# Token rows kept in f32 until they are transposed, a router that reads the residual, and a bias table and scan phases made on 128 partitions

## The chip, the cores and the metric

The kernel runs on one core of a Trainium2 chip. The core has a matrix engine (TensorE, PE; its weight loads are shown as PEld), a vector engine (VectorE, DVE), an activation engine (ScalarE, ACT), a general engine (GpSimd, POOL) and SyncE (SP), which here only issues transfers. Each engine takes its instructions in order, and semaphores hold an instruction back until what it needs is done. Sixteen DMA engines move data between the memory of the chip (DRAM) and the core. The metric is the time of one execution in microseconds (us); lower is better.

## The reference

One layer of a hybrid decoder, 512 tokens of 1,024 channels, all in f32. Cut to what matters:

```python
h = rms_norm(x, norm1_g)
proj = h @ w_in                      # 1024 -> 2048, columns split among three mixers
y_ssm  = ssm_mixer(proj[:, :256])    # complex diagonal state space, 16 groups, 64 states each, GELU, GLU
y_pool = pool_mixer(proj[:, 256:512])            # causal means over windows 2, 4, 8, 16
y_att  = moba_attention(q, k, v, rel_bias)       # 8 heads x 64, causal, with T5 bias per head and distance
x = x + concat(y_ssm, y_pool, y_att) @ w_out
h = rms_norm(x, norm2_g)
g_sel  = argmax(h @ group_w + group_b)           # one of 4 groups of experts
top2   = top_k(h @ router_w[g_sel] + router_b, 2)  # two of its 4 experts
x = x + sum over the two: weight * ((silu(h @ w_gate[e]) * (h @ w_up[e])) @ w_down[e])
out = rms_norm(x, final_norm_g)
```

The state space mixer multiplies its states by a fixed complex number per step, exp(lambda*dt). The kernel needs the powers of that number, as magnitude and phase.

## The kernel before

**Precision.** Products that must be as good as f32 are made of f16 halves: a value is kept as a high part (f16 of the value) and a low part (f16 of the rest), and three products (`PASSES`: high x high, low x high, high x low) are added in PSUM. A weight comes from DRAM as f32 into one of five staging slots (token `stg`), ACT writes the high half and DVE (sometimes POOL) the low half (`split_steps`, line 390), and the slot is free. Small things, attention and the state space are done in f32.

**Order.** Every engine's instructions stand in an order that a planner (`Flow`, lines 99 to 273) works out when the kernel is built. The work is written as generators that yield the engine, the events they need and the tokens they take; the planner holds a cost model of each instruction (lines 128 to 176) and takes, engine by engine, the piece that it believes can start first, with a rank as a handicap. A token such as `stg`, `mm` or `xT` is a place in a ring of buffers. On the chip only the order and the semaphores are left: if a transfer is slower than its model, all that stands behind the waiting instruction on that engine waits too.

**Stages.**

1. *First norm and projections* (`s_norm1`, `s_units`). x is normed, transposed on PE and split. Eight projections of 256 columns follow in the order v0, u, q0, k0, p, q1, k1, v1 (line 452). u feeds the state space, p the pooling, the others attention. `s_unit_loads` (455) brings their weights.
2. *State space* (`s_prep` 577, `s_prep_b` 633, `s_prep_e` 663, `s_prep_c` 702, `s_ssm` 905). Tokens are taken in 64 chunks of 8. DVE makes the unit's sine and cosine and then the powers 0 to 8 by complex doubling (`pw`). POOL makes the phases of chunk 0 to 63 by doubling (`eph`) and corrects their length (`nrm2`, `epn`). PE makes the chunk inputs (`pv`); DVE turns them by the phases (`z`), scans them with the magnitude `r8t`, and DVE and POOL turn them back (`unwind`). `dm` is a table that goes through DRAM (`kp_scr`).
3. *Bias table* (`s_bias`, 767). A one-hot product on PE gives a row of 639 bias values for each of 8 heads, on 8 partitions (`bv`). It is written 64 times to DRAM (`t_scr`), each copy one longer, so that reading it back with a shorter step gives every partition its row shifted by one (`tb`, eight reads). Attention (`s_attend`, 1086) needs `tb`.
4. *Clears* (`s_clear`, 800). `x_scr`, where token rows are gathered by expert slot, and the first rows of `y_scr` are written with zeros, 20 transfers of 512 KB.
5. *w_out and second norm* (`s_wout`, `x2_out`, `s_norm2` 1227). For each of four token tiles m, DVE adds the product to the residual in two halves (`x2_t[m]`); POOL and DVE multiply it by norm2_g (`xg`), PE transposes that, ACT copies it (`h2T`).
6. *Router* (`s_route`, 1265). PE makes the 20 logits; DVE scales them by the token's rms, finds the group and the two experts, and with a triangular product each token's place in its expert's 96 slots (`slot_i`). `hl_out` (1497) makes the scaled row's f16 halves, and POOL scatters these rows to `x_scr` by two indirect transfers per tile. The 16 x 96 slots are 12 units of 128. For units 0 and 1 (`NG = 2`) DVE also makes one-hot matrices (`sel`), and PE gathers the rows, already transposed, from the halves on the core (`gather`: banks `gb` for unit 0, `gc` for unit 1).
7. *Experts* (`s_xt`, `s_gate_up`, `s_down`). From unit 2 on a unit's rows are read back (`xr`), transposed on PE as 16 f16 blocks, and copied to `xT`. The gate and up products follow (`pg`), then silu, a transpose, the down product (`py`), and a scatter to `y_scr`. Expert weights come in a stream of 512 KB loads; the pages into which they are split are freed by earlier stages and units (`GU_FREE`, `DN_FREE`, events such as `dstart`).
8. *End*: rows of `y_scr` are added to the residual, normed and written.

Of the kernel before, what the change touches and what calls it, by code (L numbers as in the profile page):

```python
# [19 lines left out]
P = 128  # L20
# [13 lines left out]
NB = 32  # L34
TW = 576
# [28 lines left out]
C_W = C_JUNK + 12  # L64

# [210 lines left out]
def hybrid_trunk_kernel(tc, a, out, cap=CAPACITY, dbg=None):  # L276
# [6 lines left out]
    NG = 2  # L283
# [30 lines left out]
    x_scr = dram.tile([NSLOT + 2 * S, 2 * D], F16, name="x_scr")  # L314
# [5 lines left out]
    t_scr = dram.tile([8, HD * (VW + 1)], F32, name="t_scr")  # L320
# [44 lines left out]
    rbias = gp_.tile([P, 20], F32, name="rbias")  # L365
    ap_ = pool_of(phE, "ap_", 1, "right")
# [44 lines left out]
    def s_first_loads():  # L411
# [14 lines left out]
        sp.dma_start(spar, a["ssm_par"])  # L426
        sp.dma_start(sd, a["ssm_dl"])
# [121 lines left out]
    def cmul_p(rr, ii, ar, ai, br, bi, shape, nai=None, nbi=None):  # L549

        t_ = shaped(tmp_p, shape)
        tt = pool.tensor_tensor
        tt(t_, ai, bi, ALU.mult)
        tt(rr, ar, br, ALU.mult)
        tt(rr, rr, t_, ALU.subtract)
        tt(t_, ai if nai is None else nai, br, ALU.mult)
        tt(ii, ar, bi if nbi is None else nbi, ALU.mult)
        tt(ii, ii, t_, ALU.add)

# [5 lines left out]
    eph = (s1a[:, 0:512].rearrange("p (g c) -> p g c", g=GH), s1b[:, 1152:1664].rearrange("p (g c) -> p g c", g=GH))  # L565
    epn = prep.tile([P, 2, GH, NCH], F32, name="epn")
    nrm2 = prep.tile([P, GH, NCH], F32, name="nrm2")
# [9 lines left out]
    def s_prep():  # L577
        dt, ar_dt, th, er, r8, n_, thr, absn, us, uc = (sm() for _ in range(10))
# [3 lines left out]
        v.tensor_tensor(ar_dt, are, dt, ALU.mult)  # L582
        v.tensor_tensor(th, aim, dt, ALU.mult)
        yield "act"
        act.activation(er, ar_dt, AF.Exp)
        act.activation(r8, ar_dt, AF.Exp, scale=float(T))
        yield "dve"
        magic = 12582912.0
        v.tensor_scalar(n_, th, 1.0 / (2 * PI), magic, ALU.mult, ALU.add)
        v.tensor_scalar(n_, n_, -magic, None, ALU.add)  # L590
        c1 = 6.28125
        c2 = float(np.float32(2 * PI - c1))
        v.scalar_tensor_tensor(thr, n_, -c1, th, ALU.mult, ALU.add)
        v.scalar_tensor_tensor(thr, n_, -c2, thr, ALU.mult, ALU.add)
        lim = 3.1415925
        v.tensor_scalar(thr, thr, lim, -lim, ALU.min, ALU.max)
        v.scalar_tensor_tensor(absn, thr, -1.0, thr, ALU.mult, ALU.max)
        yield "act", ("rs",)
        act.activation(us, thr, AF.Sin)
        act.activation(uc, absn, AF.Sin, bias=hpi, scale=-1.0)  # L600
        e1["unit"] = (uc, us)
        e1["r8"] = r8
        fl.sig("unit")

        m2, t_, wre, wim, lm1, ire, iim = (sm() for _ in range(7))
# [7 lines left out]
        yield "dve"  # L613
        v.memset(pw[:, 0, 0, :], 1.0)
        v.memset(pw[:, 1, 0, :], 0.0)
        v.tensor_tensor(pw[:, 0, 1, :], er, uc, ALU.mult)
        v.tensor_tensor(pw[:, 1, 1, :], er, us, ALU.mult)
        for n in (1, 2, 4):
            yield "dve"
            cmul(pw[:, 0, n + 1:2 * n + 1, :], pw[:, 1, n + 1:2 * n + 1, :],  # L620
                 pw[:, 0, 1:n + 1, :], pw[:, 1, 1:n + 1, :],
                 pw[:, 0, n:n + 1, :].to_broadcast([P, n, GH]),
                 pw[:, 1, n:n + 1, :].to_broadcast([P, n, GH]), [n, GH])
# [39 lines left out]
    def s_prep_e():  # L663

        yield "pool"
        pool.memset(bbd, 0.0)
        yield "pool", ("unit", "rs")
        er_, ei_ = e1["unit"]
        for _ in range(3):
            yield "pool"  # L670
            nr, ni = sm(), sm()
            cmul_p(nr, ni, er_, ei_, er_, ei_, [GH])
            er_, ei_ = nr, ni
        yield "pool"
        pool.memset(eph[0][:, :, 0:1], 1.0)
        pool.memset(eph[1][:, :, 0:1], 0.0)
        n = 1
        while n < NCH:
            yield "pool"
            cmul_p(eph[0][:, :, n:2 * n], eph[1][:, :, n:2 * n], eph[0][:, :, 0:n], eph[1][:, :, 0:n],  # L680
                   bc3(er_, n), bc3(ei_, n), [GH, n])
            if 2 * n < NCH:
                yield "pool"
                nr, ni = sm(), sm()
                cmul_p(nr, ni, er_, ei_, er_, ei_, [GH])
                er_, ei_ = nr, ni
            n *= 2
        fl.sig("eph")
        tt = pool.tensor_tensor
        t_ = shaped(tmp_p, [GH, NCH])  # L690
        yield "pool"
        tt(nrm2, eph[0], eph[0], ALU.mult)
        tt(t_, eph[1], eph[1], ALU.mult)
        tt(nrm2, nrm2, t_, ALU.add)
        yield "dve"
        v.tensor_scalar(nrm2, nrm2, -1.0, 2.0, ALU.mult, ALU.add)
        yield "pool"
        tt(epn[:, 0], eph[0], nrm2, ALU.mult)
        tt(epn[:, 1], eph[1], nrm2, ALU.mult)
        fl.sig("epn")  # L700
# [197 lines left out]
    def v_out(ps, b, t):  # L898
        yield "act"
        act.activation(v_sb[:, t, b * 256:(b + 1) * 256], ps[:, 0:256], AF.Copy, scale=ISC)  # L900
        fl.give("mm")
        fl.sig(("v", b, t))


    def s_ssm():
        XT = {"wa": xs_[0], "wb": xs_[1], "zt": xs_[2], "U": xs_[3], "glw": xs4}

# [1184 lines left out]
```

## Time and profile before

| | us |
|---|---|
| median of three runs | 452.4 |
| lowest and highest of them | 450.56, 454.28 |
| profiled execution, its own time | 451.55 |
| its span, first to last instruction | 449.7 |
| mean granted PE clock in it | 0.933 |

| engine | busy us | instructions |
|---|---|---|
| PE | 377.0 | 3,472 |
| DVE | 321.9 | 655 |
| ACT | 245.9 | 397 |
| POOL | 106.0 | 183 |

| what moves | |
|---|---|
| in all | 109.84 MB, mean 244 GB/s |
| read from DRAM, written to it | 83.56 MB, 25.67 MB |

Busy time is an average over stages with different limits. A busy engine is not the bound by itself: what counts is which wait ends last in a stage. Nearly every instruction has line 91, the helper that records it, so a group is known by its tiles: `px<-wo,cat` is the w_out product, `pg<-gu,xts` an expert's gate and up product. The tile names are those of the buffer's first owner (`xp` is the page of x, later used by the scan, the residual and the rows that are scattered; `sm_r` holds the router's small values).

A row of a timeline reads: start, length, engine, line, operation, written tile, read tiles, shape, count of merged instructions, and in brackets the idle time of that engine before it and who ended it. A row of waits reads: who waited, for whom, us in total, times, the longest.

### The profile page before, as it was taken

To read this page: it belongs to the slowest core of one execution; us is meant where nothing else is said; L and a number is where in the kernel's file an instruction comes from. 1 tells how busy PE (TensorE), PEld (TensorE's weight loads), DVE (VectorE), ACT (ScalarE), POOL (GpSimd) and SP (SyncE) were. 2 spreads that over 40 slices of the span, in tenths; PEclk is the share of its full clock that TensorE was granted. 3 is DMA by queue.
4 is the path that set the end of the run, shared out by engine and by line. 5 is a ranking of instruction groups with operands and counts; after the bars stand their busy time and mean duration, and the time that the engine had idled before them with its cause. 6 is when DMAs were issued, how large, how long until landed. Compare 5 with 4: busy or idle time off the path is not lost. (4 is left out here: it accounts for less than half of the span.)

```text
span 449.7 us, 8913 instructions
## 1 busy us (share of the span) xinstructions
PE 377.0 (84%) x3472; PEld 209.2 (47%) x3472; DVE 321.9 (72%) x655; ACT 245.9 (55%) x397; POOL 106.0 (24%) x183
## 2 busy tenths in 40 slices
PE   2899963399998999999899758989999796596992
PEld 1697531164445556444455556545444342242341
DVE  2789805955673786788589998488877786796382
ACT  4752203143564994876677423387667777475131
POOL 1248985402300000000325561010302002000010
PEclk9999995779999999999999967999999898598997
DMA  8912548996796389675477697547899997989943
GB/s 279 348 50 38 73 51 222 382 383 218 238 143 209 99 247 390 211 233 188 140 232 279 253 353 288 185 149 218 276 415 364 377 361 284 316 284 339 349 164 142
DMA packets 48816, 109.84 MB, mean 244 GB/s; under 512 B 4195, under 2 KB 25443, under 8 KB 48772
## 3 DMA queue, kind: packets, MB, share of 16 engines
q1 hardware_dynamic: 45620, 99.57, 68.8%
q0 software_dynamic: 2592, 9.44, 5.2%
q8 instruction: 28, 0.46, 0.4%
q10 hardware_dynamic: 560, 0.25, 0.3%
q14 instruction: 16, 0.13, 0.1%
HBM read 83.56 MB, written 25.67 MB: 243 GB/s over the span
## 5 line engine op out<-in xcount | busy, mean ns | idle before, releaser
L91 DVE SCALAR_TENSOR_TENSOR gu<-st_lde,gu 128x1024 f16<-128x1024 f32 x56 | 69.4, 1255 | 16.9 <-ACT gu L91 16.8
L91 PE MATMUL pg<-gu,xts 128*32 128x512 f16 (+1 forms) x912 | 65.3, 395 | 7.1 <-ACT gu L91 7.0
L91 ACT ACTIVATE gu<-st_lde 128x1024 f16<-128x1024 f32 x56 | 58.4, 1055 | 23.2 <-DMA st_lde<-in_moe_w_gate_dram 13.8
L91 PEld LDWEIGHTS <-xts 128*32 128x32 f16 (+1 forms) x912 | 28.1, 102 | 40.2 <-issue 17.1
L91 PE MATMUL px<-wo,cat 128*128 128x512 f16 x192 | 44.9, 379 | 0.8 <-DVE xp L91 0.8
L91 PE MATMUL py<-dn,aT 128*32 128x512 f16 (+1 forms) x480 | 39.4, 413 | 4.6 <-ACT aT L91 3.2
L91 DVE SCALAR_TENSOR_TENSOR dn<-st_lde,dn 128x1024 f16<-128x1024 f32 x31 | 37.1, 1218 | 3.0 <-ACT dn L91 2.8
L91 POOL DMA_INDIRECT y_scr<-ys,tok x10 | 12.3, 1234 | 103.1 <-ACT ys L91 82.7
L91 ACT ACTIVATE dn<-st_lde 128x1024 f16<-128x1024 f32 x32 | 33.7, 1058 | 3.9 <-DMA st_lde<-in_moe_w_down_dram 3.4
L91 PEld LDWEIGHTS <-hT 128*64 128x64 f16 (+1 forms) x384 | 31.3, 156 | 7.0 <-issue 2.7
L91 PE MATMUL ps_k<-hT,w_k 128*128 128x512 f16 x96 | 23.3, 395 | 10.8 <-ACT qk L91 10.8
L91 ACT ACTIVATE pr<-pr,nm 128x128 f32<-128x128 f32 (+3 forms) x32 | 17.9, 559 | 23.7 <-DVE nm L91 23.4
L91 POOL TENSOR_TENSOR xg<-xp,g 128x512 f32<-128x512 f32 x4 | 6.1, 1513 | 97.2 <-DVE nm L91 92.7
L91 PEld LDWEIGHTS <-cat 128*128 128x128 f16 x192 | 18.2, 99 | 22.8 <-issue 4.9
L91 PEld LDWEIGHTS <-aT 128*32 128x32 f16 (+1 forms) x480 | 14.5, 105 | 25.8 <-issue 6.6
L91 PE MATMUL ps_v<-w_v,hT 128*128 128x256 f16 x192 | 25.3, 290 | 0.9 <-ACT hT L91 0.5
L91 ACT COPY pts<-ptp 128x128 f32<-128x128 f32 (+3 forms) x32 | 13.3, 423 | 19.7 <-PE ptp L91 19.4
L91 PE MATMUL psS<-qk 64*64 64x128 f32 (+3 forms) x128 | 23.9, 472 | 0.0
L91 PE MATMUL ptp<-cpk,pr 128*128 128x128 f32 x80 | 14.4, 288 | 10.0 <-DVE rcp L91 7.4
L91 PE MATMUL ps_q<-hT,w_q 128*128 128x512 f16 x96 | 22.7, 379 | 0.0
L91 PEld LDWEIGHTS <-w_k 128*128 128x128 f16 x96 | 9.2, 100 | 23.1 <-issue 13.9
L91 PEld LDWEIGHTS ptp<-cpk,pr 128*128 128x128 f32 x80 | 9.4, 142 | 18.2 <-issue 12.6
(265 smaller groups left out, 721.5 us busy)
## 6 DMA issues: line engine op xcount, KB each, us to landing
st_lde<-in_moe_w_down_dram SPq DMA_DIRECT2D x32, 512.0 KB
st_lde<-in_moe_w_gate_dram SPq DMA_DIRECT2D x28, 512.0 KB
st_lde<-in_moe_w_up_dram SPq DMA_DIRECT2D x28, 512.0 KB
x_scr<-zero SPq DMA_DIRECT2D x12, 512.0 KB
xr<-x_scr SPq DMA_DIRECT2D x10, 512.0 KB
xp<-in_x_dram SPq DMA_DIRECT2D x8, 512.0 KB
y_scr<-zero SPq DMA_DIRECT2D x8, 512.0 KB
yr<-y_scr SPq DMA_DIRECT2D x4, 1024.0 KB
```

Source lines behind the costliest of these rows:

```text
L91: r = f(*args, **kw)
```

## The change

*Bias table.* The one-hot product's left side is widened to 8 heads x 16 copies, so that the table stands on all 128 partitions. It is written once (16 copies per head), and eight reads of 16 partitions each fill `tb`. The loads of `small` and `pool_w` move behind the write.

*Scan phases.* `s_prep` works out the phase of every chunk and the magnitude and phase of every power from one product: the step's angle in turns, split into an exact high part and a rest, times a row of multipliers (`mul`, 73 columns: 0 to 63, then 0 to 8 eighths), reduced to half a turn, then one sine and one cosine on ACT over 584 columns. The doubling on DVE and on POOL, `nrm2` and `epn` go; the unwinding uses the same phases. Projection p waits for `bl` instead of `cl`, and the mixer's gate weights are loaded ahead (`s_glw`).

*Clears.* The planner takes one at a time (token `clr`), from the start of projection u instead of k0.

*Router.* The transposes read `x2_t` itself; norm2_g is multiplied into the router's weights (`rw`). DVE makes the scaled row once, in f32, over the residual (`s_xs`); that row is scattered as it is, so `x_scr` holds f32 rows of the same 4 KB. Slots are worked out before the one-hot matrix, and the scatter is its own piece (`s_scatter`).

*Units.* Only unit 0 is gathered on PE (`NG = 1`), by eight f32 products per tile. Unit 1 is read back like the later ones, into the residual page of the last tile. Transposed blocks are f32, and the halves are split after the transpose (`parts_out`: ACT the high, DVE the low part). All units use two `xT` buffers in turn.

```diff
-    NG = 2
+    NG = 1
...
-    x_scr = dram.tile([NSLOT + 2 * S, 2 * D], F16, name="x_scr")
+    x_scr = dram.tile([NSLOT + 2 * S, D], F32, name="x_scr")
...
-    t_scr = dram.tile([8, HD * (VW + 1)], F32, name="t_scr")
+    t_scr = dram.tile([1, 8 * NC * (VW + 1)], F32, name="t_scr")
...
+        x, y = (w.rearrange("p (g c) -> p g c", g=GH) for w in (scr_b[:, 0:GH * NPH], s1b[:, 1152:1152 + GH * NPH]))
+        mulb = mul.unsqueeze(1).to_broadcast([P, GH, NPH])
         magic = 12582912.0
...
+        v.tensor_tensor(x, mulb, bc3(uh, NPH), ALU.mult)
+        v.tensor_scalar(y, x, magic, None, ALU.add)
+        v.scalar_tensor_tensor(x, y, -magic, x, ALU.add, ALU.subtract)
+        yield "dve"
+        v.tensor_tensor(y, mulb, bc3(ul, NPH), ALU.mult)
+        v.tensor_tensor(x, y, x, ALU.subtract)
+        v.tensor_scalar(y, x, magic, None, ALU.add)
+        v.scalar_tensor_tensor(x, y, -magic, x, ALU.add, ALU.subtract)
+        v.scalar_tensor_tensor(y, x, -1.0, x, ALU.mult, ALU.max)
         yield "act", ("rs",)
...
+        act.activation(ph[1], x, AF.Sin, scale=-TURN)
+        act.activation(ph[0], y, AF.Sin, bias=hpi, scale=-TURN)
+        fl.sig("unit", "eph")
...
     def s_prep_e():
-
         yield "pool"
         pool.memset(bbd, 0.0)
-        yield "pool", ("unit", "rs")
...
-        while n < NCH:
-            yield "pool"
-            cmul_p(eph[0][:, :, n:2 * n], eph[1][:, :, n:2 * n], eph[0][:, :, 0:n], eph[1][:, :, 0:n],
-                   bc3(er_, n), bc3(ei_, n), [GH, n])
...
+        v.tensor_copy(rbx.rearrange("p (h c) -> p h c", c=NC), rb.unsqueeze(2).to_broadcast([NB + 1, 8, NC]))
...
-            pe.matmul(pb[0:8, 0:c1 - c0], rb, oh[:, c0:c1], start=True, stop=True)
+            pe.matmul(pb[:, 0:c1 - c0], rbx, oh[:, c0:c1], start=True, stop=True)
...
-        sp.dma_start(t_scr.rearrange("h (p w) -> h p w", p=HD), bv.unsqueeze(1).to_broadcast([8, HD, VW + 1]))
+        sp.dma_start(t_scr[0].rearrange("(p w) -> p w", w=VW + 1), bv)
...
+        for j in range(2):
+            for r in range(0, HD, NC):
+                sp.dma_start(tb[j * HD + r:j * HD + r + NC], bass.AP(
+                    t_scr.tensor, t_scr.offset + j * NC * (VW + 1) + HD - 1 - r,
+                    [[VW, NC], [2 * NC * (VW + 1), NPAIR], [1, TW]]))
...
+            yield "sp", ("zero", ("start", "u")), ("clr",)
...
+        v.tensor_tensor(rw, rw, g2c.unsqueeze(2).to_broadcast([P, KD, 20]), ALU.mult)
...
-                pe.transpose(pt[:, i * P:(i + 1) * P], xg[:, k * P:(k + 1) * P], ident)
+                pe.transpose(pt[:, i * P:(i + 1) * P], x2_t[m][:, k * P:(k + 1) * P], ident)
...
+    def s_xs(m, rs16):
+
+        yield "dve", ("rest",) + ((("acc", m), ("h2T", m, 1)) if m < NT - 1 else ())
+        xs = xs_m[m] = x2_t[m] if m < NT - 1 else M["R"].tile([P, D], F32, name="xs3")
+        for nh in range(2):
+            if nh:
+                yield "dve"
+            half = slice(nh * 512, (nh + 1) * 512)
+            v.scalar_tensor_tensor(xs[:, half], x2_t[m][:, half], rs16, g2_t["g"][:, half], ALU.mult, ALU.mult)
+        fl.sig(("xs", m))
+
+    def parts_out(u, h, ps, end):
+
+        yield "act"
+        hi, lo = (xT_[u][:, i * KD + 4 * h:i * KD + 4 * h + 4, :] for i in range(2))
+        src = ps.rearrange("p (k n) -> p k n", k=4)
+        act.copy(hi, src)
+        yield "dve"
+        v.tensor_tensor(lo, src, hi, ALU.subtract)
+        end()
...
+            pe.matmul(M["gb"][k // 4][:, (k % 4) * P:(k % 4 + 1) * P], src[:, k], M["sel"][:, m, 0],
+                      start=(m == 0 and k % 4 == 0), stop=(m == NT - 1 and k % 4 == 3))
...
-    DN_FREE = ("prep", "s1", ("end", "k1"), ("end", "v1"), ("wo_end", 0), ("gather", NG - 1, NT - 1), ("gup", 1))
+    DN_FREE = ("prep", "s1", ("end", "k1"), ("end", "v1"), ("wo_end", 0), ("gather", 0, NT - 1), ("xT", 1))
...
+            yield "sp", (("B",) if u > NG else ()) + tuple(("scatd", m) for m in range(NT)) + (("acc", NT - 1),), ("xr",)
+
+            xr = x2_t[NT - 1] if u == NG else B["ex"].tile([P, D], F32, tag="xr", name=f"xr{u}")
             sp.dma_start(xr, x_scr[u * P:(u + 1) * P, :])
```

`hl_out`, `gather`, `gathered` and `s_gather_all` go.

More of the change, by code (lines that the diff above doesn't have):

```diff
@@ L34 @@
 NB = 32
+NC = 16
+NPH = NCH + T + 1
 TW = 576
@@ L564, in hybrid_trunk_kernel @@
     bb = prep.tile([P, 2, GH, H], F32, name="bb")
[L565 to L567 removed]
+    ph = [prep.tile([P, GH, NPH], F32, name=f"ph{i}") for i in range(2)]
+    eph = [x[:, :, 0:NCH] for x in ph]
+    mag = prep.tile([P, GH, T + 1], F32, name="mag")
+    mul = prep.tile([P, NPH], F32, name="mul")
     r8t = prep.tile([P, GH, NCH], F32, name="r8t")
@@ L595, in s_prep, with halves @@
-        lim = 3.1415925
-        v.tensor_scalar(thr, thr, lim, -lim, ALU.min, ALU.max)
-        v.scalar_tensor_tensor(absn, thr, -1.0, thr, ALU.mult, ALU.max)
-        yield "act", ("rs",)
[L599 to L605, printed above, removed]
+        def halves(hi, x):
+            v.tensor_scalar(t_, x, 4097.0, None, ALU.mult)
+            v.tensor_tensor(u_, t_, x, ALU.subtract)
+            v.tensor_tensor(hi, t_, u_, ALU.subtract)
@@ L902, in v_out, with s_glw @@
         fl.sig(("v", b, t))
+    GLW = []
+    def s_glw():
+        yield "sp", ("rs", ("start", "k0"))
+        GLW.append(xs4.rearrange("p (a b) -> p a b", a=2))
+        for gp in range(2):
+            sp.dma_start(GLW[0][:, gp, :], a["glu_w"][gp])
+        fl.sig_dma("glw")
     def s_ssm():
@@ L969, in s_ssm @@
         fl.sig("sprev")
-        glw = sw([P, 2, 256], "glw")
-        for gp in range(2):
-            sp.dma_start(glw[:, gp, :], a["glu_w"][gp])
-        fl.sig_dma("glw")
+        glw = GLW[0]
         y_sb = sw([P, T, GH, H], "zt")
@@ L1411, in s_gather @@
[L1411 to L1432 removed]
+    xs_m = {}
@@ new lines, in unit_end, with end, s_gather @@
+    def unit_end(u, h, tag, left):
+        def end():
+            fl.give(tag)
+            left[0] -= 1
+            if not left[0]:
+                fl.sig(("xT", u))
+        return end
+    def s_gather(m):
+        yield "pe", ((("sel", m - 1), ("gather", 0, m - 1)) if m else (("wo_end", 1),)) + (("xs", m),), () if m else ("mm", "mm")
+        if m == 0:
+            M["gb"] = [bank("mm", f"gb{i}") for i in range(2)]
+        src = xs_m[m].rearrange("p (c k) -> p k c", k=KD)
+        for k in range(KD):
+            if k == 4:
+                yield "pe"
+            pe.matmul(M["gb"][k // 4][:, (k % 4) * P:(k % 4 + 1) * P], src[:, k], M["sel"][:, m, 0],
+                      start=(m == 0 and k % 4 == 0), stop=(m == NT - 1 and k % 4 == 3))
+        fl.sig(("gather", 0, m))
+        if m == NT - 1:
+            xT_[0] = xts[0]
+            left = [2]
+            for h in range(2):
+                fl.spawn(0, parts_out(0, h, M["gb"][h], unit_end(0, h, "mm", left)))
@@ L1434, in unit_in @@
     def unit_in(u):
-        return xts[(u - 1) % NXT]
+        return xts[u % NXT]
     def s_gates():
```

296 lines of the change are left out of this document (95 added, 201 removed).

## The prediction

> **What bounds the kernel now.** I read the busy table of the page, then busy time by stretch, then the waits, then each engine's timeline where TensorE (PE) stood still.
> ```profile
> PE 377.0 (84%) x3472; PEld 209.2 (47%) x3472; DVE 321.9 (72%) x655; ACT 245.9 (55%) x397; POOL 106.0 (24%) x183
> ```
>
> PE is busy for 84% of the span, so the question is which of its pauses the change can touch. Two lie early. In the stretches below the columns are the stretch, its length, the busy time and count of PE, PEld, DVE, ACT and POOL, then PE's granted clock, the DMA share and GB/s.
>
> ```profile
> 41.00:69.00 28.00, 22.91 (x232) 13.41 (x231) 13.29 (x12) 6.37 (x11) 25.49 (x50) 0.99 0.52 70
> 63.90:74.70 10.80, 0.03 (x2) 0.02 (x1) 2.19 (x3) 2.65 (x4) 9.38 (x9) 0.70 0.67 147
> 74.70:82.70 8.00, 8.00 (x32) 3.09 (x31) 7.95 (x12) 1.23 (x1) 1.18 (x2) 0.76 1.04 322
> 82.70:90.10 7.40, 0.03 (x1) 0.00 (x0) 7.22 (x14) 1.58 (x5) 4.08 (x3) 0.68 1.09 385
> 90.10:101.00 10.90, 10.85 (x62) 7.12 (x62) 5.72 (x14) 4.67 (x12) 0.14 (x2) 0.75 1.09 384
> ```
>
> PE is empty for 10.8 and 7.4 us, and in the two working stretches beside these it is granted only about three quarters of its clock. The waits between 56 and 92 us, and SP's between 35 and 80, say who is late:
>
> ```profile
> ACT w_p L91 <- DMA st_ld_p<-in_w_in_dram: 14.8, 2, 13.4
> DVE nrm L91 <- POOL nrm L91: 14.3, 1, 14.3
> PE ps_k L91 <- ACT qk L91: 10.8, 1, 10.8
> PE ptp L91 <- DVE rcp L91: 7.4, 1, 7.4
> SPq L91 <- DMA t_scr<-scr: 21.9, 1, 21.9
> ```
>
> The engine timelines give the chains:
>
> ```profile
> 58.56 5.35 PE L91 MATMUL ps_k<-hT,w_k 128*128 128x512 f16 x24
> 40.71 0.86 SPq L91 DMA_DIRECT2D t_scr<-scr  x1
> 41.68 5.50 SPq L91 DMA_DIRECT2D st_ld_p<-in_w_in_dram  x2
> 69.12 5.10 SPq L91 DMA_DIRECT2D tb<-t_scr  x8
> 74.05 0.58 ACT L91 ACTIVATE qk<-ps_k 128x512 f32<-128x512 f32 x1
> 71.83 2.27 POOL L91 TENSOR_TENSOR epn<-s1b,nrm 128x512 f32<-128x512 f32 x1
> 76.59 0.68 DVE L91 TENSOR_TENSOR xp<-pv,s 128x512 f32<-128x512 f32 x1
> 80.18 2.33 DVE L91 TENSOR_TENSOR_SCAN xp<-r8t,xp 128x512 f32<-128x512 f32 x2
> 85.78 1.62 DVE L91 TENSOR_TENSOR xp<-xp,xp 128x504 f32<-128x504 f32 x1
> 87.32 0.28 DVE L91 CUSTOM_DVE_ANT_0 pr<-psS,tb 128x128 f32<-128x128 f32 x1
> ```
>
> First pause: the bias rows, on 8 partitions and repeated 64 times (1,280 KB), are written from 40.71 and have landed when SP issues the tb reads at 69.12: 28.4 us. With them the 16 DMA engines are busy for 0.52 of the time at 70 GB/s. The weights of projection p, issued at 41.68, come out behind them; ACT has their split ahead of the copy of ps_k in its order, stands for 13.4 us, and copies ps_k only at 74.05; PE waits 10.8 us for that bank. Second pause: POOL's doubling of the scan phases ends with epn at 71.83+2.27 = 74.1. Only then does DVE turn pv into z, scan and unwind, 76.59 to 87.40, and the first softmax row (87.32) stands behind that in DVE's order; PE waits 7.4 us for its probabilities.
>
> The third place is the router, from the last w_out product to the first expert product:
>
> ```profile
> 252.11 1.46 PE L91 MATMUL px<-wo,cat 128*128 128x512 f16 x6
> 270.73 1.33 PE L91 MATMUL gb<-sel,hl 128*128 128x128 f16 x11 [3.65 <-DVE sel L91]
> 273.75 4.13 PE L91 MATMUL gc<-sel,xp 128*128 128x128 f16 x48
> 277.72 1.06 PE L91 MATMUL gc<-sel,hl 128*128 128x128 f16 x16
> 278.71 5.36 PE L91 MATMUL pg<-gu,xts 128*32 128x512 f16 x96
> 260.00:270.00 10.00, 5.26 (x71) 4.80 (x71) 9.55 (x34) 1.73 (x1) 6.33 (x8) 0.67 0.99 355
> ```
>
> Between 253.57 and 278.71, 25.1 us, DVE is full (9.55 of 10) and PE is not: DVE sets this stage, and at its end 5 us go to the gather of unit 1 (gc).
>
> **The change, part by part.** *Bias table.* The rows are made on 128 partitions (8 heads by 16 copies): 320 KB in place of 1,280, from 128 source partitions instead of 8. The product that makes them has the same 512 columns, so PE pays the same; DVE gets one 33x128 copy more, about 0.3 us. How long the new write takes no row shows. Bounds: at the 70 GB/s of the old one, 320/70 = 4.7 us; at the 322 of a busy stretch, 1.0 us and the wait to land. Either way tb can be read by 46 and is there near 52, before k0's first bank is full (58.56+5.35 = 63.9), so I take the whole pause of 10.8 us as gone; low end, 8 us, should the p weights still be behind something. What is late next is nothing of the bias: PE has k0's second half (5.4 us), then p.
>
> *Scan phases.* POOL's chain goes; DVE makes phases and powers at once, on 584 columns. A 512-wide product of two tensors took 0.68 us (row above), so 0.78 at 584; 8-wide ones and a one-input one took
>
> ```profile
> L91 DVE TENSOR_TENSOR sm<-sm,sm 128x8 f32<-128x8 f32 x3 | 0.5, 165 | 0.0
> L91 DVE COPY r8t<-sm 128x512 f32<-128x512 f32 x1 | 0.4, 419 | 0.0
> ```
>
> Added: six wide two-input (6 x 0.78), two one-input (2 x 0.48) and 19 small ones (19 x 0.165): 8.8 us. Removed: 29 small ones, 4.8 us, and the nrm step, 0.4. DVE pays 3.6 us net between 22 and 42 us, ACT about 0.7 for wider sines, SP 0.43 for the new multiplier row. The cover is projection u and q0 on PE to 56.5, and the first bm product may come later by 2 us without being waited for. If the cover fails it costs 3.6. For that, phases are ready near 34 instead of 74.1; z, scan and unwind (10.8 us of DVE, which now waits 14.3 us for POOL in just this stretch) run right after pv, which ends where k0 begins, at 58.6, and are done near 69.4, when k0's second half is still on PE. So the second pause goes: 7.4 us; low end 3, if the first softmax still meets the unwind.
>
> *Clock.* 18.9 us of work ran at 0.76 and 0.75; without pauses it loses at most 18.9 x 0.245 = 4.6 us less, at least 0. I take 3.5, since the pauses stand directly ahead of both stretches.
>
> By the Trainium skill (TensorE: Matmul & The Clock Gate, What's actually happening), the clock falls to one half after an idle window of about 3.4 us. The 0.70 and 0.68 of the two empty stretches agree in kind; by that rule all 4.6 us would return, 1 us more than I take.
>
> *Clears, loads.* The 20 zero writes move from behind the tb reads to single ones after projection u starts, in SP's order between the loads; bytes are unchanged and the DMA share there is 0.52. A load behind one of them is 512 KB/385 GB/s = 1.4 us late: 0 to 1.4, I take 1. small and pool_w, and glu_w, move within SP's order: nothing waits for them.
>
> *Router.* Transposes read the residual; norm2_g is folded into rw (one small DVE product, long before). On the path of the last token tile:
>
> ```profile
> 256.47 0.68 DVE L91 TENSOR_TENSOR xg<-xp,g 128x512 f32<-128x512 f32 x1
> 259.88 2.07 DVE L91 SCALAR_TENSOR_TENSOR xp<-xg,sm_r,xp 128x1024 f16<-128x1024 f32 x1
> 264.30 0.35 DVE L91 SCALAR_TENSOR_TENSOR sel<-cpk,sm_r,sel 128x128 f16<-128x128 f32 x1
> 271.90 1.29 DVE L91 TENSOR_TENSOR hl<-xg,hl 128x640 f16<-128x640 f32 x1
> 99.17 0.38 PE L91 MATMUL pk<-s,bbd 128*32 128x128 f32 x2
> 99.39 0.38 PE L91 MATMUL pk<-s1b,bbd 128*32 128x128 f32 x2
> ```
>
> Per tile DVE loses xg (0.68), the low part (2.07) and the second selection (about 0.8 with its offset), and gains the scaled rows (two halves at 0.7): 2.1 us less, three to four times, of which two tiles stand before the last tile's logits: 4 us off the path. The last tile's low part (1.29) goes too, but the low half of xT is now a DVE subtraction after ACT's copy, about +1. The gather is f32: an f32 product of 128 columns is a pair of records, 0.22 us from pair to pair (99.17 to 99.39), so 8 take 1.8 us, or 3.5 at half clock, against 2.05 now: 0 to +1.5, I take +1. gc, from 273.75 to the first expert product at 278.71, 5.0 us, leaves the path. Sum: 4 + 0.7 + 1.3 + 5.0 - 1 - 1 = 9.
>
> By the Trainium skill (FP8 and Floating Point Precision, TensorE Precision Notes) a true f32 product makes four passes through the array, which speaks against this step: 8 products would be 32 passes against 16 now, an estimate of twice the present 2.05 us, and the sum of the router would be 8 in place of 9. The pk rows agree with it in kind: two records for each f32 product.
>
> Unit 1 now comes through memory: the scatter of the last tile, a read of 512 KB, eight transposes, four half copies. The scatter's issues took two of these:
>
> ```profile
> 275.22 0.95 POOL L91 DMA_INDIRECT x_scr<-hl,slot_i  x1 [0.19 <-issue]
> 280.00:290.00 10.00, 10.00 (x126) 5.62 (x118) 5.48 (x17) 4.49 (x7) 0.00 (x0) 1.00 0.45 154
> 360.00:370.00 10.00, 9.96 (x126) 4.45 (x126) 8.37 (x10) 6.98 (x9) 0.00 (x0) 1.00 0.99 360
> ```
>
> About 2 us to issue, some 3 to land (estimate: twice 1.4 us for the bytes), 3 to read, 1 and 2.5 to turn and split: 11.5 us after the slots, which are known some 5 us before xT of unit 0. Unit 0's products (5.36) cover the rest to about 1 us. I take 1.5 lost, 0 to 6.
>
> Later units: transposes 8 f32 for 16 f16, equal on PE; DVE +0.7 each, in a stage where it has some of every 10 us free (8.37 busy at 360): 1 us in all. The weight stream is saturated at 360 us (0.99) but not at 280 (0.45), where it waits for pages that the units free: it moves with them.
>
> Sum: 10.8 + 7.4 + 3.5 - 1 (clears) - 2 (front, cover partly thin) + 9 - 1.5 - 1 = 25.2 us. The profiled execution took 451.55 us (span 449.7), which would become 426.4; the median of the runs is 452.4, so 427.
>
> **The rivals.** (1) *Unit 1 is late*: its read stands in SP's order behind a weight load that waits for a slot, and the router's 9 us are given back. The SP timeline has such a block right there, 15.7 us:
>
> ```profile
> 267.66 15.74 SPq L91 DMA_DIRECT2D st_lde<-in_moe_w_gate_dram  x2
> ```
>
> Against it: that block ended with slots that the end of gc frees, and gc goes. Time: 427 + 9 = 436. (2) *DVE becomes the front's bound*: the softmax still waits behind splits and scan, only the bias pause goes, with half the clock: 452.4 - 10.8 - 1.8 + 1 = 441. For it: DVE is 7.95 of 8 busy from 74.7; against it: those 14.3 us in which it waits for POOL. (3) *The change does nothing for the end*: the expert stage keeps its own end because its weight stream is the bound: 452. Against it, the share of 0.45. (4) *Slower*: copying xT in ACT-then-DVE pairs makes it late in every unit. From transposes to both halves is 1 + 2.5 us; with 11 units exposed 3.5 us each, 38 us: 427 + 38 = 465. It decides against the change from 30 us, 2.7 per unit. Against it: the two xT buffers remain, and PE waited 1.4 us in all before the ten units' transposes, the last column of this group's row:
>
> ```profile
> L91 PE MATMUL tx<-tri,xr 128*128 128x128 f16 x160 | 11.3, 220 | 1.4 <-ACT xts L91 1.4
> ```
>
> **How the numbers follow.** My forecast has 0.55, unit 1 late 0.16, DVE-bound front 0.13, no effect 0.08, slower 0.08. The likeliest is 427. Its own range is 415 (all ends good: 25.2 with 1.1 more of clock and the 5.5 of losses gone make 31.8; and 5.6 more in the router, whose DVE is full now) to 434 (low ends of both pauses). The range for 8 in 10 reaches to the second rival: 415 to 441. Differences under 1% cannot be told from none here: faster 0.84, same 0.08, slower 0.08.
>
> **What would show it.** The wait of SP for t_scr should fall from 21.9 to under 6; PE's pauses of 10.8 and 7.4 should be gone and the clock full from 60 to 100; the last w_out product should end near 233 rather than 253.6; from there to the first expert product 16 us rather than 25.1, with no gap before unit 1. The prediction is wrong if a new PE pause over 5 us stands in the front, or if the expert stage takes longer from its first product to the end than now (278.7 to 449.7, 171 us).

## The result, and the profile after

| | us |
|---|---|
| changed kernel, median of 4 runs (lowest, highest) | 437.25 (435.2, 438.06) |
| kernel before, beside it, median of 4 runs | 451.48 |
| ratio, 95% interval | 0.968 (0.961 to 0.975) |
| profiled execution after: its own time, its span | 435.2, 433.2 |

The kernel is 14 us faster by the medians and 16.4 by the two profiled executions (451.55 to 435.2). The forecast was 25, the range reached from 415 to 441. First the busy table of the page of the changed kernel:

```profile
PE 381.7 (88%) x3336; PEld 214.4 (49%) x3336; DVE 321.1 (74%) x650; ACT 236.3 (55%) x400; POOL 50.7 (12%) x86
```

POOL has lost half its work, the other engines hardly anything: what was won is waiting. Busy time by stretch of the changed kernel, with the same columns as before (stretch, length, PE, PEld, DVE, ACT, POOL, PE's clock, DMA share, GB/s); the last row runs from the last w_out product to the first expert product:

```profile
60.00:80.00 20.00, 14.62 (x123) 7.26 (x122) 19.64 (x28) 6.18 (x11) 5.18 (x6) 0.93 1.01 294
63.90:101.00 37.10, 31.60 (x179) 15.16 (x177) 28.09 (x70) 13.94 (x38) 8.52 (x12) 0.95 0.53 161
...
237.98:258.85 20.87, 18.76 (x109) 18.22 (x108) 12.71 (x61) 2.12 (x5) 8.96 (x17) 0.84 0.94 354
```

Before, the stretch from 63.9 to 101 held the two pauses, at clocks from 0.68 to 0.76. Now PE works for 31.6 of the 37.1 us, at 0.95. PE's timeline of the changed kernel says what is left of the pauses there, and gives the marks at the other end of the row above:

```profile
48.75 0.63 PE L96 MATMUL ptb<-cpk,bl 128*128 128x128 f32 x4 [1.42 <-DVE bl L96]
65.67 0.87 PE L96 MATMUL psS<-qk 64*64 64x128 f32 x8 [0.69 <-ACT qk L96]
77.81 0.48 PE L96 MATMUL ptp<-cpk,pr 128*128 128x128 f32 x1 [4.70 <-DVE pr L96]
...
235.23 2.75 PE L96 MATMUL px<-wo,cat 128*128 128x512 f16 x12
246.06 6.06 PE L96 MATMUL gb<-sel,xp 128*128 128x128 f32 x24
254.83 4.09 PE L96 MATMUL gb<-sel,xs 128*128 128x128 f32 x16 [2.11 <-DVE sel L96]
258.85 5.36 PE L96 MATMUL pg<-gu,xts 128*32 128x512 f16 x96
...
271.89 1.16 PE L96 MATMUL tx<-cpk,xp 128*128 128x128 f32 x8
274.53 1.13 PE L96 MATMUL tx<-cpk,xr 128*128 128x128 f32 x8 [1.48 <-DMA xr<-x_scr]
275.59 5.37 PE L96 MATMUL pg<-gu,xts 128*64 128x512 f16 x48
```

The wait of 10.8 us ahead of k0's second half is gone. The one ahead of the first probabilities (`ptp`) is 4.7 us where it was 7.4. The last w_out product ends at 235.23 + 2.75 = 237.98, 15.6 us earlier than before; from there to the first expert product it takes 20.9 us instead of 25.1; unit 1's product begins 16.7 us after unit 0's, where it was 7.2 us. DVE's timeline around the pause that stayed:

```profile
61.00 1.35 DVE L96 TENSOR_TENSOR s1b<-spar,pw 128x1152 f32<-128x1152 f32 x1
...
65.05 1.35 DVE L96 TENSOR_TENSOR s<-spar,npw 128x1152 f32<-128x1152 f32 x1
66.32 2.48 DVE L96 TENSOR_TENSOR xp<-pv,ph 128x512 f32<-128x512 f32 x4
68.71 1.28 DVE L96 TENSOR_TENSOR xp<-xp,xp 128x512 f32<-128x512 f32 x2
69.91 0.28 DVE L96 CUSTOM_DVE_ANT_0 pr<-psS,tb 128x128 f32<-128x128 f32 x1
70.31 2.33 DVE L96 TENSOR_TENSOR_SCAN xp<-r8t,xp 128x512 f32<-128x512 f32 x2
72.69 1.46 DVE L96 TENSOR_TENSOR xp<-xp,ph 128x504 f32<-128x504 f32 x1
...
75.75 1.62 DVE L96 TENSOR_TENSOR xp<-xp,xp 128x504 f32<-128x504 f32 x1
77.29 0.15 DVE L96 RECIPROCAL rcp<-smx 128x1 f32<-128x1 f32 x1
```

DVE is full here (19.64 of the 20 us from 60 to 80, the first row above). First come four products of the state space's output table (`cl`, in the pages s1b, scr and s), then the turning of pv (66.32), the first softmax row (69.91), scan and unwind; only at 77.29 is that row's sum turned into a factor, and PE gets it.

### The profile page after: what moved, and what is told of

Its sections match the earlier page's. It is cut to its first block, busy times and chain, and to the rows that moved or that the text cites. A ratio compares the mean times of both kernels' runs of the same rounds, so it can differ in the third digit from the quotient of the medians.

```text
span 433.2 us, 8564 instructions
## 1 busy us (share of the span) xinstructions
PE 381.7 (88%) x3336; PEld 214.4 (49%) x3336; DVE 321.1 (74%) x650; ACT 236.3 (55%) x400; POOL 50.7 (12%) x86
## 5 line engine op out<-in xcount | busy, mean ns | idle before, releaser
L96 PE MATMUL pg<-gu,xts 128*32 128x512 f16 (+1 forms) x960 | 71.4, 397 | 6.6 <-ACT gu L96 6.6
L96 DVE SCALAR_TENSOR_TENSOR gu<-st_lde,gu 128x1024 f16<-128x1024 f32 x56 | 67.4, 1219 | 11.0 <-ACT gu L96 10.6
L96 PEld LDWEIGHTS <-xts 128*32 128x32 f16 (+1 forms) x960 | 31.0, 103 | 42.3 <-issue 16.8
L96 PE MATMUL py<-dn,aT 128*32 128x512 f16 (+1 forms) x480 | 40.9, 443 | 6.6 <-ACT aT L96 5.8
L96 DVE SCALAR_TENSOR_TENSOR dn<-st_lde,dn 128x1024 f16<-128x1024 f32 x32 | 38.5, 1220 | 6.3 <-ACT dn L96 6.1
L96 ACT ACTIVATE dn<-st_lde 128x1024 f16<-128x1024 f32 x32 | 33.4, 1058 | 4.3 <-DMA st_lde<-in_moe_w_down_dram 4.2
L96 PEld LDWEIGHTS <-cat 128*128 128x128 f16 x192 | 18.2, 98 | 22.3 <-issue 3.6
L96 DVE CUSTOM_DVE_ANT_0 pr<-psS,tb 128x128 f32<-128x128 f32 (+3 forms) x32 | 15.6, 486 | 14.8 <-PE psS L96 14.7
L96 POOL DMA_INDIRECT y_scr<-ys,tok x10 | 10.5, 1047 | 124.2 <-ACT ys L96 124.2
L96 PE MATMUL ptp<-cpk,pr 128*128 128x128 f32 x80 | 14.4, 285 | 7.8 <-DVE pr L96 7.8
L96 POOL TENSOR_TENSOR sm_r<-ss 128x1 f32<-128x1 f32 x4 | 3.6, 901 | 123.0 <-ACT xs L96 123.0
L96 ACT ACTIVATE ys<-py,cw 128x512 f32<-128x512 f32 (+1 forms) x14 | 9.6, 686 | 15.2 <-PE py L96 13.5
```

The lines of the kernel that those rows point to most:

```text
L96: r = f(*args, **kw)
```

## The experiments

For each profiled execution four marks in us: when the last w_out product ended, the first expert product began, the load of expert 8's gate weights went out (from there on the weight stream is dense), and the span. The last column is the expert stage, from its first product to the end.

```
                            w_out end  first expert  expert 8 load   span   stage
before                        253.57      278.71        311.80      449.7   171.0
changed                       237.98      258.85        295.19      433.2   174.4
p1 bias table alone           255.29      280.30        313.40      452.2   171.9
p2 scan phases alone          257.34      283.75        316.85      452.4   168.7
p3 front alone                240.98      265.85        298.95      440.7   174.9
p4 router and units alone     256.72      278.56        313.91      448.5   169.9
q1 read of unit 1 first       238.31      259.76        294.47      430.7   170.9
q2 four splits on GpSimd      239.14      260.35        293.72      434.7   174.4
q3 scan ahead of table        238.59      260.55        295.00      430.1   169.6
q4 places ahead of gather     238.06      258.33        294.47      430.0   171.7
r1 changed, again             240.44      261.52        297.53      435.8   174.3
r2 gather of 16 bits          238.81      252.53        289.15      424.6   172.1
r3 q1 and q4                  238.90      259.68        294.40      432.0   172.3
r4 q1, q3 and q4              234.27      254.42        289.84      426.0   171.6
```

Two profiles of the same program (changed, r1) differ by 2.5 us at the end of w_out, and over all rows the expert stage's length spreads over 6 us, so single profiles settle a question only where they differ by more; the ratios decide the rest. The kernel before ran beside each of the three groups p, q and r; the changed kernel ran beside r only (0.965) and in the first measurement (0.968), so small differences between a q and the changed kernel stay uncertain.

**The parts, alone.** p1 takes the hunks of `s_bias` and `t_scr`, p2 those of `s_prep`, `s_prep_e`, the unwinding and projection p's wait for `bl`, p3 both with the clears and the gate load (these two were not tried apart), p4 all that concerns `x_scr`, the router and the units.

> The kernel before with the new bias table alone. Theory: the two pauses of the front lie one behind the other but do not add. The scan phases on POOL still end near 74 us, and scan and unwind stand ahead of the first softmax on DVE, so the wait of 10.8 us before k0's second half goes and most of it comes back in the wait before the first transposed probabilities (7.4 us before, 13 to 18 here). The last w_out product ends 0 to 4 us earlier than 253.6, and the whole is 0 to 5 us faster (447 to 452). Rival, the sum as predicted: the pauses add, 10.8 us less and some clock, 438 to 441.

> The kernel before with the scan phases on DVE alone. Theory: PE still waits 10.8 us for the p weights behind the bias rows, and in that wait DVE, no longer held by POOL, does scan and unwind; the second pause (7.4 us) goes. The last w_out product ends 6 to 9 us earlier (245 to 248), the whole is 5 to 9 us faster (443 to 447). Rival: DVE is the bound of the front, so the phases that it now makes itself push everything behind them, and the gain is under 3 us.

> Bias table, scan phases, clears and the early gate load together; router and units as before. Theory: the front's gain is that of the changed kernel, the last w_out product ends near 238 (15 to 16 us earlier), the stage from there to the first expert product is 25 us as before, and the expert stage 171: 435 to 438. Then all of the gain is the front's and the router's part adds nothing to the end. Rival: the router's 4 us reach the end in the changed kernel, and this one is 4 us slower than it: 440 to 442.

> Router and units alone (f32 rows, residual transposed, unit 1 through memory); the front as before. Theory: the first expert product comes 4 us sooner after the last w_out product (21 us instead of 25), and the expert stage gives 3 to 4 us back before the load of expert 8's gate weights, so the whole is within 2 us of before (449 to 453). Rival, the sum as predicted: 9 us less up to the first expert product and 2.5 lost after it, 444 to 446.

| | ratio to before | 95% interval |
|---|---|---|
| p1, bias table | 0.999 | 0.994 to 1.004 |
| p2, scan phases | 1.015 | 1.009 to 1.021 |
| p3, both with clears and gate load | 0.971 | 0.965 to 0.976 |
| p4, router and units | 0.989 | 0.982 to 0.996 |

Each half of the front alone is worth nothing, or less; together they are worth 13 us. PE's timeline of p1 and then of p2 shows why:

```profile
78.08 2.74 PE L96 MATMUL ps_k<-hT,w_k 128*128 128x512 f16 x6 [13.53 <-DVE xp L96]
89.60 0.90 PE L96 MATMUL ptp<-cpk,pr 128*128 128x128 f32 x3 [2.42 <-DVE pr L96]
```

```profile
93.17 0.48 PE L96 MATMUL ptp<-cpk,pr 128*128 128x128 f32 x1 [17.18 <-DVE pr L96]
```

In p1 the table comes early, yet k0's second half starts 3.4 us later than before: it now waits 13.53 us for a bank of PSUM (the memory that PE writes to) that pv holds until DVE turns it, and DVE, ahead of the turning in its order, has a step that waits 13.66 us for POOL's chain. That step and the turning in DVE's timeline of p1:

```profile
70.13 0.43 DVE L96 TENSOR_SCALAR nrm<-nrm 128x512 f32<-128x512 f32 x1 [13.66 <-POOL nrm L96]
...
76.14 0.68 DVE L96 TENSOR_TENSOR xp<-pv,s 128x512 f32<-128x512 f32 x1
```

The place was right in the expectation (the scan takes over), the waiting instruction was not: the bank, before the softmax is reached. In p2 it is the other way round. DVE is done with scan and unwind in time, and the first softmax row waits for `tb`, here in DVE's timeline of p2 and then in SP's:

```profile
88.81 0.29 DVE L96 CUSTOM_DVE_ANT_0 pr<-psS,tb 128x128 f32<-128x128 f32 x1 [11.05 <-DMA tb<-t_scr]
```

```profile
51.17 0.86 SPq L96 DMA_DIRECT2D t_scr<-scr  x1
...
72.88 7.60 SPq L96 DMA_DIRECT2D x_scr<-zero  x2
80.58 7.46 SPq L96 DMA_DIRECT2D tb<-t_scr  x8
```

The `tb` reads go out from 80.58 on, 11.5 us later than before (69.12), because the repeated write itself goes out 10.5 us later (51.17, where it was 40.71). DVE's timeline of the kernel before and then of p2 shows its copies of the bias rows, which the write needs:

```profile
38.56 0.68 DVE L91 COPY scr<-pb 8x512 f32<-8x512 f32 x1
...
40.42 0.27 DVE L91 COPY scr<-pb 8x127 f32<-8x127 f32 x1
```

```profile
49.66 0.67 DVE L96 COPY scr<-pb 8x512 f32<-8x512 f32 x1
50.86 0.28 DVE L96 COPY scr<-pb 8x127 f32<-8x127 f32 x1 [0.54 <-PE pb L96]
```

In p2 they stand behind the new phases, the split of w_k and the first products of `bl`. At the old 28.4 us the write would have landed at 79.6 (an estimate), so the two zero writes of 512 KB ahead of the reads in SP's order account for about 1 us at most. So p2 is not the price of the new phases alone: they also delay the old write. The 17.18 us are nearly both old pauses together (10.8 + 7.4 = 18.2). The expectation, 5 to 9 us won, was wrong: it left out that the softmax needs the late table too. So the two chains ran side by side (before, POOL's phases ended at 74.1 and the `tb` reads went out from 69.12 to 74.2); a gain shows only when both are shortened. p3 lies between its theory and its rival: its median of 440.4 us is in the rival's range, its ratio of 0.971 is 0.3 to 0.6% above the changed kernel's 0.968 and 0.965; its w_out ended 3 us later than expected. p4 gave 4.9 us by its ratio, between theory and rival: its first expert product comes 21.8 us after w_out instead of 25.1, and its stage is no longer than before. The product of p3 and p4 is 0.960, that of the whole 0.968 and 0.965 in its two measurements, so the parts nearly add.

**What holds unit 1 and expert 8.** In the changed kernel SP's timeline has unit 1's read (`xp<-x_scr`) behind two weight loads that wait for slots:

```profile
261.78 0.33 SPq L96 DMA_DIRECT2D st_lde<-in_moe_w_gate_dram  x1
265.82 0.34 SPq L96 DMA_DIRECT2D st_lde<-in_moe_w_up_dram  x1
266.28 0.36 SPq L96 DMA_DIRECT2D xp<-x_scr  x1
```

q1 makes these loads wait for the read's issue; q2 moves four of eight weight splits (the low halves of experts 5 and 6's gate and up weights) from DVE to POOL.

```diff
             sp.dma_start(xr, x_scr[u * P:(u + 1) * P, :])
             fl.sig_dma(("xr", u))
+            fl.sig(("xi", u))
...
+                if (e, i, j) == (7, 0, 1):
+                    need += (("xi", NG),)
```

```diff
-  e < 8 and less_busy(1.0), left, ...
+  e < 8 and (less_busy(1.0) or (e in RAW and i < 2 and j == 1)), left, ...
```

> The changed kernel with the reads of unit 1 and unit 2 issued ahead of the two weight loads that wait for slots (SP's order only). In the changed kernel unit 1's read was issued at 266.28, its products began at 275.59 and the load of expert 8's gate weights went out at 295.19, 36.35 us after the first expert product (33.1 before). Theory A, the late read is what costs those 3 us: unit 1's products begin 5 to 8 us earlier, expert 8's load 3 to 6 us earlier, and the whole ends with it, ratio to before 0.955 to 0.962. Theory B, DVE sets expert 8's load, because the low halves of the turned units stand among the splits that free the slots: unit 1's products begin earlier all the same, expert 8's load within 1.5 us of 295.2, ratio 0.965 to 0.970.

> The changed kernel with four of the eight low halves of experts 5 and 6's gate and up weights made by GpSimd instead of DVE; the order of SP's loads up to expert 8 is nearly the same. DVE gets 4 x 1.22 = 4.9 us of work less between the first down product (267.5) and expert 8's load (295.2). Theory B (DVE's splits set that load): it goes out 3 to 5 us earlier, 290 to 292, and the end comes with it, ratio to before 0.957 to 0.962. Theory A (unit 1's late read sets it): no change, 295 and 0.967; or slower, if GpSimd's slower splits come late.

q1: ratio 0.961 (0.956 to 0.965). The read goes out at 262.98 instead of 266.28, but unit 1's products begin at 274.86, only 0.7 us earlier. SP's waits in q1 say what the read now waits for, and the page's table of DMA issues (of the changed kernel, then of before) how long a scatter takes to land:

```profile
SPq L96 <- DMA x_scr<-xs,slot_i: 17.5, 1, 17.5
```

```profile
x_scr<-xs,slot_i POOLq DMA_INDIRECT x2, 7.1
```

```profile
x_scr<-hl,slot_i POOLq DMA_INDIRECT x2, 4.2
```

The last tile's scatter takes 7.1 us to land where it took 4.2, and behind the read PE's order has the whole down product of unit 0 ahead of unit 1's transposes. The blocked read was real and cost next to nothing. The ratio lies in A's range, but without the marks that A needs, and r3 below, which adds this step to q4, is no faster than q4 (0.959 and 0.958). Theory A has fallen; expert 8's load came 0.7 us earlier, as B had it, though the ratio is below B's range.

q2: ratio 0.969 (0.964 to 0.973). Expert 8's load comes 33.4 us after the first expert product instead of 36.3: DVE's splits do set it, as B said, although on the profile's own clock it goes out only 1.5 us earlier (293.72) and not at 290 to 292. But the end does not come with it; the stage is 174.4 us, as in the changed kernel. B holds for that load and fails for the end.

The table bears on what both took for granted. From the first expert product to expert 8's load it is 33.1 us in all four kernels with the old units and 33.4 to 36.6 with the new ones. The stage as a whole, though, is 171.6 us in the mean of the four old ones and 172.1 in the mean of the ten new ones: on average the delay does not reach the end. But single kernels lie anywhere from 168.7 to 174.9, and the changed kernel's own two profiles lie high (174.4 and 174.3, where before was 171.0), with as much time behind expert 8's load as before (138.0 and 138.3, against 137.9). A cost of 3 us in the changed kernel is neither shown nor ruled out.

**The pause that stayed.** q3 holds the six products of the output table back until the scan is done.

```diff
-        yield "dve"
+        yield "dve", ("scan",)
         v.tensor_tensor(td, ci, pi_, ALU.mult)
...
+        fl.sig("scan")
         L = NCH - 1
```

> The changed kernel with the six products of the state space's output table (cl) held back until the scan is done, so that the turning of pv stands ahead of them on DVE. The output table and what hangs on it (pk, kp_scr, dm, py) come later. Theory: the second pause, 4.70 us before the first transposed probabilities, was DVE's order; it falls below 1.5 us, and the last w_out product ends 2 to 5 us earlier than 237.98, ratio to before 0.957 to 0.964. Rival: the 4.7 us are hidden work of DVE, which is full from 60 to 80 us; the pause goes, but the same time comes back as small waits later in the front, and the last w_out product ends within 1.5 us of 238.

PE's timeline of q3:

```profile
74.78 0.33 PE L96 MATMUL ptp<-cpk,pr 128*128 128x128 f32 x1 [1.43 <-DVE pr L96]
```

The pause fell to 1.43 us. The last w_out product ended at 238.59, which is the rival; but the same order of the front ended at 234.27 in r4. The medians of r4 and r3 (r4 without this step), which ran side by side, are 5 us apart, 429.5 and 434.6, and q3's ratio of 0.952 (0.947 to 0.956) lies below both of the changed kernel's. So it is a gain of a little over 1%, but not by the marks that the theory named, and where it is realised stays open.

**The gather in f32.** q4 only moves the product that gives the last tile's places (`pc3`) ahead of the third tile's gather in PE's order: DVE had waited 2.85 us for it.

```diff
-  ... + (("xs", m),), () if m else ("mm", "mm")
+  ... + (("xs", m),) + ((("pc", NT - 1),) if m == 2 else ()), () if m else ("mm", "mm")
...
+        fl.sig(("pc", m))
```

> The changed kernel with the place product of the last tile (pc3) ahead of the third tile's gather in PE's order; nothing else moves. In the changed kernel DVE waited 2.85 us for that product while PE worked through f32 gathers. Theory: the one-hot matrices are ready 2 to 2.5 us earlier, the first expert product comes 18.4 to 19 us after the last w_out product instead of 20.87, and expert 8's load and the end come 1 to 2.5 us earlier, ratio 0.962 to 0.966. Rival: the path is PE's, 64 f32 gathers at some 0.25 us; the third tile's gather then ends later and the last one begins no earlier, 20.5 to 21 us.

r2 is q4 with the gather in f16, on the upper 16 of each value's 32 bits only. It leaves out the lower half of every value of unit 0 and reads the upper half as f16, so unit 0's rows are not the layer's; it is a run for the time alone.

```diff
-  M["sel"] = M["R"].tile([P, NT, NG, P], F32, name="sel")
+  M["sel"] = M["R"].tile([P, NT, NG, P], F16, name="sel")
...
-        src = xs_m[m].rearrange("p (c k) -> p k c", k=KD)
+        src = xs_m[m].bitcast(F16).rearrange("p (c k h) -> p h k c", k=KD, h=2)[:, 1]
```

> The kernel of q4 (place product ahead of the third tile's gather) with the gather of unit 0 in f16: it takes only the upper 16 bits of each f32 value, so unit 0's rows lack their lower part. Same number of products, 32 of 128x128x128. Theory: the f32 price of these products (0.5 us each, 16 us in all) is what holds the router's stage in q4 (20.3 us); in f16 they cost at most 0.13 us each, the last gather starts when the one-hot matrix is ready (14.5 us after the last w_out product), and the first expert product comes 16 to 17 us after it, the 16 us of the prediction. Expert 8's load comes 3 to 4 us earlier than in q4 (290.5 to 291.5). Rival: another engine takes over (copies and subtractions to xT on ACT and DVE), under 1.5 us gained.

PE's timeline of q4 and then of r2:

```profile
250.12 4.17 PE L96 MATMUL gb<-sel,xp 128*128 128x128 f32 x16
254.09 0.40 PE L96 MATMUL pcnt<-hot,one 128*128 128x16 f16 x8
254.34 4.06 PE L96 MATMUL gb<-sel,xs 128*128 128x128 f32 x16
258.33 1.91 PE L96 MATMUL pg<-gu,xts 128*32 128x512 f16 x32
```

```profile
248.11 0.17 PE L96 MATMUL pc<-hot,tri 128*128 128x16 f16 x1 [4.72 <-DVE hot L96]
...
251.26 1.01 PE L96 MATMUL gb<-sel,xs 128*128 128x128 f16 x8 [1.18 <-DVE sel L96]
252.53 6.75 PE L96 MATMUL pg<-gu,xts 128*32 128x512 f16 x96 [0.25 <-ACT xts L96]
```

In q4 the one-hot matrix is there 2.3 us earlier, but PE is still in the third tile's gather and goes from gather to gather: the stage is 20.3 instead of 20.9 us, next to the rival's 20.5 to 21. The ratio is 0.958 (0.952 to 0.964), lower than 0.6 us in this stage accounts for; the rest is not explained. In r2 a tile's gather costs 1.0 us instead of 4.1, PE waits for DVE again (4.72 us for `hot`), and the stage takes 13.7 us, less than the 16 to 17 expected. Expert 8's load follows (289.15), and so does the whole: 0.946 (0.938 to 0.953), 428.2 us beside 437.4 of r1 and 434.6 of r3.

**Together.**

> The changed kernel itself, beside the others of this call, so that the single steps can be compared with it on the same chip. Expected ratio to before 0.967 (0.960 to 0.975, its interval).

> The changed kernel with both clean moves of order, q1 (reads of units 1 and 2 ahead of two weight loads) and q4 (place product ahead of the third tile's gather). Theory: with the slots known 2.3 us earlier the last scatter lands 2 us earlier, near 261, and now the read can follow it: unit 1's products begin 1 to 3 us earlier than in q4 (272 to 274). If DVE's splits set expert 8's load it stays within 1 us of 294.5 and the ratio is that of q4, 0.955 to 0.961; if unit 1 sets it, 292 to 293 and 0.952 to 0.957.

> The changed kernel with q1, q3 and q4 together. q3 (scan ahead of the output table) did not end w_out earlier, yet its whole was 5 us shorter. Theory: that part is a difference between chips and profiles, for nothing in its trace up to expert 8's load is earlier; then this is as r3, within 0.5%. Rival: the other order of splits and loads that q3 brings shortens the weight stream after expert 8 (92.4 us instead of 94.9), and this kernel is the fastest, 0.945 to 0.952.

r1: 0.965 (0.957 to 0.973), 437.4 us. r3: 0.959 (0.951 to 0.967), 434.6 us; unit 1's products began at 274.78 and not at 272 to 274 as expected, and expert 8's load stayed at 294.40. r4: 0.948 (0.936 to 0.959), 429.5 us, the fastest that computes the whole layer; q1, q3 and q4 are changes of order alone. The time is the rival's, the theory's "as r3" is not. The rival's cause, a shorter weight stream, is not what the marks show: w_out and the first expert product were early already.

## Why the prediction was right in its sign and 10 us too far

By its terms, against the profiles:

- *First pause, 10.8 us: right.* SP's timeline of the changed kernel:

```profile
50.15 0.35 SPq L96 DMA_DIRECT2D t_scr<-scr  x1
52.38 4.02 SPq L96 DMA_DIRECT2D tb<-t_scr  x8
```

  The new write took 2.2 us, between the bounds of 1.0 and 4.7. It went out 9.4 us later than the old one, much as in p2, and the reads went out 6 us later than the forecast of 46; the short write hides it. That the two pauses were added was right only because both parts were made: p1 and p2 show that neither stands alone. The text priced each as if it were its own gain, and did not see that pv holds a bank that k0 needs; that adding them came out near the truth was luck.
- *Second pause, 7.4 us: mis-sized.* 2.7 came, just under its low end of 3. The step that failed is "z, scan and unwind [...] run right after pv": pv was done at 63.6, the turning began at 66.32 behind the table's products, and unwind ended at 77.4. The prediction named DVE's order as the cause of the old pause and did not ask what else of DVE's would be moved into the same place. In q3, which turns pv first, the pause is 1.43 us.
- *Clock, 3.5 us: right in kind.* 0.95 in the stretch that had 0.68 to 0.76; what that gave in us was not measured. Nor did a run take the clears (1 us) and the thin cover (2 us) apart from the rest.
- *The front's end.* 237.98 and 240.44 in two profiles; the terms (18.7 us) would give 234.9, the text said 233. The 4.7 us of the pause that stayed are of the size of the difference (3.1 and 5.5), but that it is the cause is not shown: without it w_out ended at 238.59 in q3 and at 234.27 in r4.
- *Router, 9 us: 4.3 came; the step that failed is the price of the f32 gather.* It was taken from an f32 product whose stationary side had 32 columns, 0.22 us, and only the last tile's eight products were charged, +1. In the gather 16 records, two for each product, take 4.09 us, so 0.51 a product, and all 32, 16 us, stand in the 20.9 us in which DVE had been the bound. It is not the clock: eight products took 3.89 us from 237.82, granted 1.00, and 4.09 from 254.83, granted 0.61. The profile's groups in the changed kernel (busy time, mean ns of one, then the idle time before it):

```profile
L96 PE MATMUL gb<-sel,xp 128*128 128x128 f32 x48 | 12.1, 418 | 0.0
L96 PEld LDWEIGHTS gb<-sel,xp 128*128 128x128 f32 x48 | 11.8, 335 | 0.1
L96 PE MATMUL gb<-sel,xs 128*128 128x128 f32 x16 | 4.1, 440 | 2.1 <-DVE sel L96 2.1
...
L96 PEld LDWEIGHTS pk<-s,bbd 128*32 128x32 f32 x16 | 1.8, 110 | 0.0
L96 PEld LDWEIGHTS pl<-rw,h2T 128*128 128x128 f32 x64 | 7.6, 192 | 0.1
```

  The weight load of a gather record takes 335 ns, that of the row the price came from 110. The width is not all of it: the router's logits (`pl`, last line) have 128 f32 columns on that side too, load in 192 ns, and eight of their products took 1.86 us (244.35), 0.23 each. Their columns lie side by side, the gather's 32 bytes apart (`p (c k) -> p k c`), and they move 20 columns against 128, which `pk` moves as well. Nor is it that layout alone: the units' transposes (`tx`) load 128 f32 columns with the same step in 194 ns and take 0.28 us each (274.53, eight records in 1.13). What of the product, its width and its layout together makes the 0.51 stays open; no run changed one of them alone. That this price held the stage is shown by r2: with the gather in f16 the stage takes 13.7 us, even less than the 16 of the forecast. The Trainium skill (FP8 and Floating Point Precision, TensorE Precision Notes) gives a true f32 product four passes, and by it the prediction worked out twice 2.05 us for the last tile and set it aside; the trace gave 4.09. As a rule for every f32 product the rows do not bear it out: `pk`'s took 0.22 us where an f16 product of the gather took 0.13.
- *Unit 1, -1.5 us, and rival 1.* The mechanism of the rival was there to the letter: its read stood behind a weight load. Its price was not 9 us but nothing that can be told from the scatter: q1 removes it and unit 1 moves by 0.7 us. The forecast of 11.5 us from slots to product was short too (22 us in the changed kernel, from the slots at 253.6 to 275.59; the scatter alone took 7.1 for an estimated 3), but no time hung on it at the end.
- *Later units, -1 us: right in kind.* DVE's copies to `xT` went from 6.8 us for ten units to 14.4 for eleven (0.63 us more for each), PE's transposes from 11.3 to 13.5; what that cost is lost in the stage's scatter (171.6 and 172.1 us in the means).
- *The other rivals.* DVE was not the front's bound; it was late in one place. The expert stage did not keep its own end: it starts earlier and ends earlier, so what is won ahead of it arrives but for at most its 3.4 us, in r2 too. The ACT-then-DVE pairs cost PE nothing in this profile: its waits ahead of the units' transposes are 1.5 us for a read, those ahead of their products 6.6 us for weights.
- *The signs it named.* SP's wait for `t_scr` fell from 21.9 to 0.3 us, and no new pause exceeds 5 us (4.7). But the first expert product came 20.9 us after w_out and not 16, there is a gap before unit 1, and one of the two signs of being wrong was there: the expert stage took 174.4 us, longer than 171.

The sum, then: 15.6 + 4.3 - 3.4 = 16.5 between the two profiled executions. Whether the 3.4, the longer expert stage, is a cost of the new units or scatter stays open.

## What to carry to other kernels

When two waits follow each other on one engine, draw both chains to their sources before adding them: if they run side by side and end at the same time, removing one gives nothing, and its test alone would have had this change thrown away. When a bound engine is relieved, add up all that the next engine does in that stretch, not only what lies on the old chain: a halved number of gathers at four times the price moved the router's bound from DVE to PE. And take the price of a product from a row that is like it in type, in both widths and in layout: here a row of the same width on the stationary side would still have said 0.23 us for 0.51.

## What the runs showed of the hardware

An f32 product of 128 x 128 x 128 took 0.51 us in the gather, an f16 one 0.13 (r2: 1.01 us for 8); an f32 transpose of the same size took 0.28 (274.53: 8 records in 1.13 us), so the type and the size alone do not give the price. Of the bias rows 320 KB from 128 partitions landed in 2.2 us, 1,280 KB repeated from 8 partitions in 28.4 us at a DMA share of 0.52: four times the bytes, thirteen times the time. Other transfers ran beside each, and what the shape alone does was not tried. A scatter of 128 rows took 7.1 us to land with the DMA engines 0.87 busy in that stretch (253.9 to 262.9), and 4.2 before at 0.48 (275.2 to 281.0); that the load is the cause was not tried.

Unwinding on DVE and POOL at once may have brought nothing: DVE's additions of two operands in SBUF, the on-core memory, took 0.64 us alone (68.71, two in 1.28) and 1.62 beside POOL's. The Trainium skill (SBUF — State Buffer, SBUF: two separate sides) says that a DVE operation with two inputs in SBUF and a POOL operation that reads SBUF exclude each other for the whole instruction. The trace agrees in kind: the pair took 4.7 us from 72.69 to 77.37, and six operations of 0.64 us on DVE alone would be 3.8, an estimate that was not run.
